# Retention heads ahead of their stick-breaking pair, and a retention head's frames in two halves with the state carried between them

## The chip, the core and the metric

One core of a Trainium2 chip runs one launch of the kernel. The metric is device time in microseconds (us), the median of several runs. TensorE (PE) multiplies matrices, VectorE (DVE) and ScalarE (ACT) do elementwise work, SyncE (SP) issues the weight loads, GpSimd (POOL) issues the other DMAs.

## What is computed

One layer of an encoder for 512 prompt frames and 32 sample frames (544 columns in all), model width 1024, in float32. A normalised input `h` is projected to: queries, keys and values of 4 retention heads (256 wide each), queries, keys and values of 8 stick-breaking heads (128 wide), a gate `rg`, and two branch gates `ga`, `gb`. Merged branches go through an output projection, and an MLP of width 4096 follows. Retention, cut to what the change touches, is

```python
scores = einsum('bihd,bjhd->bhij', q, k) * decay      # inside a chunk of 64 frames, both ways
o      = einsum('bhij,bjhe->bihe', scores, v) + einsum('bihd,bhde->bihe', q, S) * q_decay
S_new  = exp(log_gamma * L) * S + einsum('bjhd,bjhe->bhde', k * k_decay, v)
```

over chunks of 64 frames, with S starting at zero; both `o` and the last S are outputs of the branch. Since the decays multiply, the sum over earlier chunks may be taken directly from keys and values or through a carried S at any frame. A stick-breaking head has exponentials and logarithms in place of a softmax: log-sigmoids of the scores, a reversed cumulative sum over keys (a product with a triangle of -1 on TensorE), an Exp, and the product with the values.

## The kernel before

Everything is kept transposed: features on the 128 partitions, frames in columns. A float32 operand is split into a rounded high part and a rest (`split`: ScalarE copies the high part, VectorE subtracts), and a product is three TensorE products high-high, high-low, low-high (`exact`, `products`). The rounded format is float32r in the code; a plain float32 product runs in two records at a lower rate and is used for blocks of 128 columns.

Weights come as 128 x 1024 tiles, in the order of their use. `load_w` loads one and splits it into `whi` (ScalarE) and `wlo` (VectorE). `gemm` multiplies one such tile with all 544 columns, in two halves of 24 products of 272 columns each; at its start it calls `load_w` for the next tile, whose two buffers are those that the gemm before it has left.

TensorE's order is fixed by the program. The main loop issues gemms, and `Flow` interleaves chains: generators that do the attention work of a head in pieces and yield what they need next (events, PSUM banks, temporaries). `Flow` keeps its own estimate of when engines and buffers are free and lets a piece go, between two k-steps of a gemm, when it holds it to be ready. The order of VectorE and ScalarE is made by a scheduler. Every engine takes its instructions in order, so an instruction that waits holds those behind it.

The stages: first the gemms that read the unnormalised input X while the norm and `h` are made (values of stick-breaking head 0, both value tiles of retention head 0, values of stick-breaking head 1, keys of retention head 0, keys of stick-breaking head 0). Then rounds c = 0 to 3: stick-breaking heads 2c and 2c+1 (gemms, then `sb_chain`), after odd rounds a group of sample frames (`sample_chain`), then retention head c (`retention_chain` for the prompt, `ret_sample_chain` for sample frames, `state_chain` for the final state). Then the gates, 24 gemms with a Sigmoid on ScalarE; after the sixth, `flow.drain()` runs every chain to its end. Output projection and MLP follow.

Names in the steps below. `sc`, `dm`, `dec` are a head's state, its decay table and its key-decay table, loaded by POOL. In `retention_chain` the scores of a 512-frame prompt are computed as blocks of 128 keys by all later queries: 512, 384, 256 and (full precision) 128 columns wide; `pt` holds them masked, `sh`, `sl` their high and low parts, and `values_of` multiplies with the values `rv_hi`, `rv_lo`, `rv_3` in the same widths. In `state_chain`, `kd` are keys times `dec`, transposed to `kt`, and four blocks of 128 frames are multiplied with the values into one bank `sb_`. In `ret_sample_chain` `pd`, `pd_r` are the sample frames' masked scores, `qd` decayed queries, `so` the normalised result that is transposed back. `e` is a stick-breaking head's 128 x 1280 work tile.

```python
    def rstd(sums, n):                       # used by every head
            S.activation(y[:, c], ps, AF.Ln, scale=1.0 / n, bias=epsb)
            S.activation(y[:, c], y[:, c], AF.Exp, scale=-0.5)
        def silu(h, c, p):                   # the gates
            S.activation(sg[:, c], p, AF.Sigmoid)
```

Of the kernel before, what the change touches and what calls it, by code (L numbers as in the profile page):

```python
# [35 lines left out]

MLP_W = 80
OUT_ORDER = (0, 4, 1, 5, 2, 6, 3, 7)

# [6 lines left out]
def constants():  # L46
# [185 lines left out]
def trunk(ctx: ExitStack, tc: tile.TileContext, a: dict, g32):  # L232
# [11 lines left out]
    def tmp():  # L244
        return tp.tile([P, NT], F32, tag="tmp", name="tmp")
# [208 lines left out]
    def query_key_parts(x, n, copy=False):  # L454
# [8 lines left out]
        return hi, lo, last  # L463

    heads = {}

# [63 lines left out]
    with tc.tile_pool(name="xin", bufs=1, side="right") as xp:  # L530
# [54 lines left out]

        flow.wait(vt=2, rv=1, tmp=9, mm=3, at=1)
        vt0, vt1 = sb_value_tiles(), sb_value_tiles()
        rv0, rvs0 = ret_value_tiles()
# [16 lines left out]
        for k in range(KD):  # L605
# [8 lines left out]
        flow.start(value_chain(rc, rv0, P, rvs0, ("rv1", 0)))  # L614
        flow.wait(tmp=1)
        rd = tmp()
        gemm(X, lambda h, c, p: V.scalar_tensor_tensor(
            rd[:, c], p, -1.0 / (2 * D), u[0][:, c], op0=ALU.mult, op1=ALU.mult
        ))
# [6 lines left out]
        rope(X, rk0, turned, 0, 0)  # L626
        flow.give(tmp=2)
        query_key(0, 1, X, u[0])
        flow.until("h", KD - 1)
# [200 lines left out]
    def leave(c):  # L830

        users[c] = users.get(c, 0) + 1
        if users[c] == 3:
            flow.give(rk=1, rq=1, rv=1)

    def retention_chain(c, vt):
# [5 lines left out]
        pt = bigp.tile([P, PACKED], F32, tag="e", name="pt", bufs=2)  # L842
        for bi, blocks in enumerate(GROUPS):
            b_ = bank()
            for n, b in enumerate(blocks):
                _, c0, w = PIECES[b]
                for d in range(2):
                    by_blocks(b_[:, c0 : c0 + w], b, k_r[d], q_r[d], n == 0 and d == 0, d == 1)
            for b in blocks:
                _, c0, w = PIECES[b]  # L850
                o = BANKS[bi][0] + c0
                V.tensor_tensor(pt[:, o : o + w], b_[:, c0 : c0 + w], dm[:, :w], op=ALU.mult)
            flow.give(at=1)
            if bi < 2:
                flow.t = flow.pe
                yield need(at=1)
        flow.give(qk0=1, qk1=1, qk2=1, qk3=1)
# [3 lines left out]
        raw, sq = [], []  # L861
        for ei in range(2):
            ob = bank()
            values_of(ob, vt, slice(ei * P, (ei + 1) * P), parts, pt)
            raw.append(tmp())
            sq.append(tmp())
            S.copy(raw[ei][:, :SEQ], ob)
            S.activation(sq[ei][:, :SEQ], ob, AF.Square)
        flow.give(e=1, sh=1, at=1)
# [12 lines left out]
        leave(c)  # L882
# [43 lines left out]
    def state_chain(c, k, vt, vsamp, sc):  # L926

        dec = bigp.tile([P, NT], F32, tag="dec", name="dec")
        nc.gpsimd.dma_start(out=dec, in_=a["dec"][c])
        yield need(("rqk", c, 0), ("rv0", c), ("rv1", c), ("carried", c), tmp=2)  # L930
        kd = [tmp(), tmp()]
# [5 lines left out]
        for half in (blocks[:4], blocks[4:]):  # L937
# [23 lines left out]
        flow.give(at=1, tmp=2)  # L961
        yield need(at=1)
        sb_ = bank()
# [10 lines left out]
    phase = (cst[:, C_COS:C_SIN], cst[:, C_SIN:C_TRI])  # L974
    for c in range(NH):
        for h in (2 * c, 2 * c + 1):
            for w_col in (1, 0):
                if (h, w_col) != (0, 1):
                    query_key(h, w_col)
            if c == 0:  # L980
                vt = (vt0, vt1)[h]
            else:
                flow.wait(vt=1)
                vt = sb_value_tiles()
                values(H, vt, 0, vs[:, h % 4, :], ("v", h), a["o_v"][h])
            flow.start(sb_chain(h, vt))
        if c % 2:
            flow.start(sample_chain(c // 2))
        x = []
        for n, tag in enumerate(("rk", "rq")):  # L990
            if c == 0 and n == 0:
                x.append(rk0)
                continue
            flow.wait(**{tag: 1})
            x.append(rope_tiles(tag))
            rope(H, x[n], phase, c, n)
        if c == 0:
            rv, rvs = rv0, rvs0
        else:
            flow.wait(rv=1)  # L1000
# [6 lines left out]
        flow.start(ret_sample_chain(c, x[0], x[1], rvs, sc))  # L1007
        flow.start(state_chain(c, x[0], rv, rvs, sc))


# [412 lines left out]
```

## Time and profile before

| | |
|---|---|
| median of 3 runs | 1002.31 us (1002.0 to 1005.52) |
| profiled execution, device time | 1002.26 us |
| its span in the profile | 1000.5 us |
| TensorE busy | 986.7 us, 99% |
| VectorE busy | 668.0 us, 67% |
| ScalarE busy | 522.7 us, 52% |
| granted TensorE clock, mean | 0.998 |
| DMA | 102.71 MB, 103 GB/s |

A row of a timeline gives the start, the duration, engine, line and operation, output tile and inputs, and in brackets the idle time before it with what ended it. Matmuls overlap: what one costs is read from the distance of two starts, not from its duration. `Flow`'s wrapper makes line 225 the line of nearly every instruction, so rows are told apart by tile names.

### The profile page before, as it was taken

The numbers are of one execution on the slowest core, as the hardware profiler recorded it, in microseconds if no ns is written. First come the engines' busy times: TensorE is split into PE (matmuls) and PEld (weight loads), VectorE is DVE, ScalarE is ACT, GpSimd is POOL, SyncE is SP. The second block draws the span as 40 slices with busy tenths as digits, with TensorE's granted clock in tenths as the row PEclk, the third lists the DMA queues.
The fourth block names the chain that finished last, engine by engine and source line by source line (L and its number), as shares of the span: only waits on it lengthen the run. The fifth ranks groups of instructions, "written<-read, shape, count | busy, mean of one in ns | idle before, by whom it ended". The sixth has DMA issues, their size and how long they took to land.

```text
span 1000.5 us, 18622 instructions
## 1 busy us (share of the span) xinstructions
PE 986.7 (99%) x7726; PEld 969.3 (97%) x7726; DVE 668.0 (67%) x1124; ACT 522.7 (52%) x963; POOL 47.2 (5%) x80
## 2 busy tenths in 40 slices
PE   9999999999999999999999999999999999999998
PEld 9999888999999999889999999999999999999998
DVE  7968768866677576756434447974676666676782
ACT  6466756537654675564333335775464445444440
POOL 0000003001000011000000011000000000000000
PEclk9999999999999999999999999999999999999999
DMA  7232224122322135114322245232223332343312
GB/s 253 87 128 75 86 75 149 64 85 96 108 64 85 64 125 164 45 51 165 97 87 85 85 142 185 85 127 85 85 93 101 103 106 87 104 129 96 119 43 90
DMA packets 30932, 102.71 MB, mean 103 GB/s; under 512 B 4096, under 2 KB 6144, under 8 KB 30848
## 3 DMA queue, kind: packets, MB, share of 16 engines
q1 hardware_dynamic: 24768, 80.88, 25.0%
q0 software_dynamic: 6080, 20.65, 6.2%
q8 instruction: 60, 0.98, 0.4%
q14 instruction: 24, 0.20, 0.1%
HBM read 90.51 MB, written 11.01 MB: 101 GB/s over the span
## 4 chain that ended last, share of the span: by engine, by line
PE 95%; ACT 2%; DVE 2%; issue 0%; ACTq 0%; DVEq 0%
PE mm L225 70%; PE at L225 25%; ACT tmp L225 1%; PE at L384 0%; DVE sl L225 0%; ACT e L225 0%; ACT whi L225 0%; ACT L225 0%; DVE tmp L225 0%; ACT kt L225 0%; DVE sh L225 0%; DVE e L225 0%; PE at L600 0%; DVE so L225 0%; ACT st L225 0%
## 5 line engine op out<-in xcount | busy, mean ns | idle before, releaser
L225 PE MATMUL mm<-h_hi,whi 128*128 128x272 f32 x1040 | 304.5, 293 | 0.0
L225 PE MATMUL mm<-h_hi,wlo 128*128 128x272 f32 x1040 | 301.1, 290 | 0.9 <-DVE wlo L225 0.9
L225 PE MATMUL mm<-h_lo,whi 128*128 128x272 f32 x1040 | 300.3, 289 | 0.0
L225 DVE TENSOR_TENSOR wlo<-raw,whi 128x1024 fp32r<-128x1024 f32 (+1 forms) x146 | 167.6, 1150 | 125.8 <-ACT whi L225 125.0
L225 ACT CAST whi<-raw 128x1024 fp32r<-128x1024 f32 (+1 forms) x146 | 144.8, 992 | 179.3 <-PE mm L225 162.1
L225 PEld LDWEIGHTS mm<-h_hi,whi 128*128 128x128 f32 x1040 | 196.7, 189 | 1.9 <-issue 1.3
L225 PEld LDWEIGHTS mm<-h_hi,wlo 128*128 128x128 f32 x1040 | 196.3, 189 | 1.1 <-DVE wlo L225 1.1
L225 PEld LDWEIGHTS mm<-h_lo,whi 128*128 128x128 f32 x1040 | 196.9, 189 | 0.1
L225 PE MATMUL mm<-u_hi,whi 128*128 128x272 f32 x512 | 147.9, 289 | 0.0
L225 PE MATMUL mm<-u_lo,whi 128*128 128x272 f32 x512 | 147.8, 289 | 0.0
L225 PE MATMUL mm<-u_hi,wlo 128*128 128x272 f32 x512 | 147.7, 288 | 0.0
L225 PEld LDWEIGHTS mm<-u_hi,whi 128*128 128x128 f32 x512 | 96.6, 189 | 0.4 <-DVE y L225 0.2
L225 PEld LDWEIGHTS mm<-u_lo,whi 128*128 128x128 f32 x512 | 96.5, 188 | 0.0
L225 PEld LDWEIGHTS mm<-u_hi,wlo 128*128 128x128 f32 x512 | 96.3, 188 | 0.0
L225 PE MATMUL at<-f_hi,wlo 128*128 128x272 f32 x320 | 92.7, 290 | 0.0
L225 PE MATMUL at<-f_lo,whi 128*128 128x272 f32 x320 | 92.2, 288 | 0.0
L225 PE MATMUL at<-f_hi,whi 128*128 128x272 f32 x320 | 92.1, 288 | 0.0
L225 ACT ACTIVATE tmp<-tmp 128x272 f32<-128x272 f32 (+2 forms) x148 | 75.4, 553 | 29.6 <-DVE tmp L225 29.1
L225 DVE TENSOR_TENSOR y<-mm,y 128x272 f32<-128x272 f32 x112 | 48.6, 436 | 29.3 <-PE mm L225 29.3
L225 PEld LDWEIGHTS at<-f_hi,whi 128*128 128x128 f32 x320 | 60.5, 189 | 0.0
L225 PEld LDWEIGHTS at<-f_lo,whi 128*128 128x128 f32 x320 | 60.4, 189 | 0.0
L225 PEld LDWEIGHTS at<-f_hi,wlo 128*128 128x128 f32 x320 | 60.3, 188 | 0.0
(234 smaller groups left out, 1795.0 us busy)
## 6 DMA issues: line engine op xcount, KB each, us to landing
raw<-in_w SPq DMA_DIRECT2D x142, 512.0 KB, 3.5
x<-in_x SPq DMA_DIRECT2D x8, 272.0 KB, 5.2
o_v<-tmp POOLq DMA_DIRECT2D x8, 272.0 KB, 2.4
o_k<-tmp POOLq DMA_DIRECT2D x8, 272.0 KB, 2.5
x<-in_x POOLq DMA_DIRECT2D x8, 272.0 KB, 3.6
o_y<-x POOLq DMA_DIRECT2D x8, 272.0 KB, 2.4
tmp<-o_y POOLq DMA_DIRECT2D x8, 272.0 KB, 3.8
o_y<-y SPq DMA_DIRECT2D x16, 136.0 KB, 1.7
```

What stands on the lines that cost most here:

```text
L225: f(out, *args, **kw)
```

## The change

1. The order of heads is a list, `HEADS`: R0 S0 S1 R1 S2 S3 R2 S4 S5 R3 S6 S7. In the first stage, the values of stick-breaking head 1 and the keys of head 0 make way for the queries of retention head 0. The weights are packed in the new order.
2. A retention head's prompt is treated as two halves of 256 frames. Scores are made inside each half only: 256 columns for its first 128 keys, 128 full-precision ones for the second 128. The later half's queries read the state that the first half leaves: `state_chain` copies the bank after its first two blocks (`mids`), `retention_chain` splits the copy into `sh`, `sl`, multiplies it with the later queries (bank `cx`), and multiplies the result with a decay that stands in the free half of `dm`; it is added to the values' product on VectorE. The final state goes out through `kd[0]` in place of `so_p`.
3. `state_chain` no longer waits for `carried` before its key products but before its update of `sc`; `retention_chain` waits for `mid`.

```diff
+HEADS = "R0 S0 S1 R1 S2 S3 R2 S4 S5 R3 S6 S7".split()
...
+        dm[h, :, 256:] = np.exp(lg[h] * (np.arange(256) - 255))[None]
...
+    def ret_parts(x, n, key):
+
+        hi = qkp.tile([P, SEQ], F32R, tag=f"qk_hi{n}", name=f"qk_hi{n}")
+        lo = qkp.tile([P, SEQ], F32R, tag=f"qk_lo{n}", name=f"qk_lo{n}")
+        src, h, l = x[:, :SEQ], hi, lo
+        if key:
+            src, h, l = (t.rearrange("p (n c) -> p n c", c=256)[:, :, :P] for t in (src, hi, lo))
+        split(src, h, l)
+        return hi, lo, x
...
-        p = 2 - 2 * n
+        p = 2 * n
         yield need(**{f"qk{p}": 1, f"qk{p + 1}": 1})
-        heads["ret", c, n] = [query_key_parts(x[d], p + d) for d in range(2)]
+        heads["ret", c, n] = [ret_parts(x[d], p + d, n == 0) for d in range(2)]
...
-        flow.start(value_chain(rd, vt1, 0, vs[:, 1, :], ("v", 1), a["o_v"][1]))
...
+        rq0 = rope_tiles("rq")
+        rope(X, rq0, turned, 0, 1)
         flow.give(tmp=2)
-        query_key(0, 1, X, u[0])
...
+        pt = bigp.tile([P, PACKED], F32, tag="e", name="pt", bufs=2)[:, : 3 * L]
+        b_ = bank()
+        for i in range(2):
+            for d in range(2):
+                exact(
+                    b_[:, i * L : (i + 1) * L], [t[:, i * L : i * L + P] for t in k_r[d][:2]],
+                    [t[:, i * L : (i + 1) * L] for t in q_r[d][:2]], i == 0 and d == 0, d == 1, **SG,
+                )
+        decayed(b_, 0, L)
...
+                T.matmul(
+                    b_[:, i * P : (i + 1) * P], k_r[d][2][:, s], q_r[d][2][:, s],
+                    start=i == 0 and d == 0, stop=d == 1, **SG,
+                )
+        decayed(b_, 2 * L, P)
...
-        yield need(("rv0", c), ("rv1", c), sh=1, tmp=5, at=2)
-        parts = packed_parts(pt)
+        yield need(("rv0", c), ("rv1", c), ("mid", c), sh=1, tmp=5, at=3)
+        parts = [bigp.tile([P, PACKED + 2 * P], F32R, tag=t, name=t) for t in ("sh", "sl")]
+        M0 = PACKED - SEQ
+        split(mids.pop(c), *[t[:, M0:PACKED] for t in parts])
...
+        cx = bank()
+        for ei in range(2):
+            for d in range(2):
+                o = M0 + d * L + ei * P
+                exact(
+                    cx[:, ei * L : (ei + 1) * L], [t[:, o : o + P] for t in parts],
+                    [t[:, L:] for t in q_r[d][:2]], ei == 0 and d == 0, d == 1, **SG,
+                )
...
+            for b, o, w in ((0, 0, L), (2, L, L), (1, 2 * L, P)):
+                q0 = b * P
+                exact(
+                    ob[:, q0 : q0 + w], [t[:, b, cols] for t in vt[:2]], [t[:, o : o + w] for t in parts],
+                    b == 0, b == 1, **SG,
+                )
+            T.matmul(ob[:, 3 * P :], vt[2][:, cols], pt[:, 2 * L + P :], start=False, stop=True, **SG)
+            S.copy(raw[ei][:, :L], ob[:, :L])
+            V.tensor_tensor(raw[ei][:, L:SEQ], ob[:, L:], carried[:, ei, :], op=ALU.add)
...
-        yield need(("rqk", c, 0), ("rv0", c), ("rv1", c), ("carried", c), tmp=2)
+        yield need(("rqk", c, 0), ("rv0", c), ("rv1", c), tmp=2)
...
-                    [t[:, m, :] for t in vt[:2]], m == 0 and d == 0, m == 3, **SG,
+                    [t[:, m, :] for t in vt[:2]], m == 0 and d == 0, m % 2 == 1, **SG,
                 )
-        so_p = bigp.tile([P, 512], F32, tag="so_p", name="so_p")
+            if c not in mids_made:
+                mids_made.add(c)
+                mids[c] = bigp.tile([P, 512], F32, tag="so_p", name="so_p")
+                S.copy(mids[c], sb_)
+                flow.finish("mid", c)
+        so_p = kd[0][:, :SEQ]
...
-        yield need(at=1)
+        yield need(("carried", c), at=1)
...
+    for kind, n in HEADS:
+        (stick_breaking if kind == "S" else retention)(int(n))
```

What this moves, at three places. First, TensorE, round 0: the end of the first stick-breaking head's cumulative sums (`neg1_r`) and its value products (`vt_hi`, `vt_lo`; the numbers tell buffers apart). Before:

```order
L225 MATMUL at_1111<-sl_1246,tri_r_765 128x256
L225 MATMUL at_1111<-e_1112,neg1_r_767 128x128
L225 MATMUL at_1401<-tmp_r_1332,ones_r_78 128x272
L225 MATMUL at_1401<-tmp_r_1333,ones_r_78 128x272
L225 MATMUL at_1404<-tmp_r_1332,ones_r_78 128x272
L225 MATMUL at_1404<-tmp_r_1333,ones_r_78 128x272
L225 MATMUL at_1425<-tmp_r_1397,ones_r_78 128x272
L225 MATMUL at_1425<-tmp_r_1398,ones_r_78 128x272
L225 MATMUL at_1428<-tmp_r_1397,ones_r_78 128x272
L225 MATMUL at_1428<-tmp_r_1398,ones_r_78 128x272
L225 MATMUL at_1444<-sh_1421,vt_hi_187 128x512
```

Now, after 55 other rows behind the same head's `neg1_r` product:

```order
L229 MATMUL mm_1691<-h_hi_107,whi_1574 128x272
L229 MATMUL mm_1691<-h_lo_108,whi_1574 128x272
L229 MATMUL mm_1691<-h_hi_107,wlo_1575 128x272
L229 MATMUL at_1695<-sh_1625,vt_hi_187 128x512
L229 MATMUL at_1695<-sl_1626,vt_hi_187 128x512
L229 MATMUL at_1695<-sh_1625,vt_lo_188 128x512
```

Eight sums stood between the two steps of the head; now projection matmuls and the next head's scores do.

Second, VectorE after the first stage, in the changed kernel (`tmp_823`, `tmp_824` are `kd`, `wlo` a weight's low part, `at_864` the retention scores):

```order
L229 TENSOR_TENSOR qk_lo3_820<-rq1_597,qk_hi3_819 128x512
L229 TENSOR_TENSOR tmp_823<-rk0_413,dec_771 128x544
L229 TENSOR_TENSOR tmp_824<-rk1_414,dec_771 128x544
L229 TENSOR_TENSOR qd_887<-rq0_596,cst_72 128x32
L229 TENSOR_TENSOR qd_887<-rq1_597,cst_72 128x32
L229 TENSOR_TENSOR wlo_849<-raw_847,whi_848 128x1024
L229 TENSOR_TENSOR tmp_r_907<-tmp_805,tmp_r_906 128x544
L229 TENSOR_TENSOR pt_863<-at_864,dm_769 128x512
L229 TENSOR_TENSOR pd_881<-at_878,cst_72 32x32
L229 TENSOR_TENSOR kt1_897<-at_891,kt0_896 128x512
L229 TENSOR_TENSOR pd_r_882<-pd_881,pd_r_882 32x32
```

Before, the products with `dec` came after the two stick-breaking heads of round 0.

Third, ScalarE in the gates (`at_5502` to `at_5504` are the last head's scores, `mm` a gate's product, `whi_5553` the high part of the weight for the fifth gate gemm). Before:

```order
L225 CAST kt0_5472<-at_5467 128x512
L225 ACT_TABLE_LOAD
L225 ACTIVATE tmp_5479<-at_5476,epsb_80 128x512
L225 ACT_TABLE_LOAD
L225 ACTIVATE tmp_5479<-tmp_5479 128x512
L225 ACTIVATE tmp_5480<-tmp_5479 128x512
L225 COPY so_p_5512<-at_5414 128x512
L225 ACT_TABLE_LOAD
L225 ACTIVATE tmp_5435<-mm_5442 128x272
```

Now:

```order
L229 ACTIVATE e_5505<-at_5503 128x512
L229 ACTIVATE e_5505<-at_5504 128x256
L229 ACT_TABLE_LOAD
L229 ACTIVATE e_5505<-e_5505 128x1280
L229 ACT_TABLE_LOAD
L229 ACTIVATE tmp_5436<-mm_5489 128x272
L229 ACT_TABLE_LOAD
L229 ACTIVATE e_5505<-e_5505 128x1280
L229 CAST whi_5553<-raw_5552 128x1024
L229 ACT_TABLE_LOAD
```

From the first gate to the end of the chains there were 4 table loads and there are 13.

## Rows read from the trace of the kernel before

**Rows 1.** The page, part 1: busy us, share of the span and instructions of each engine.

```profile
PE 986.7 (99%) x7726; PEld 969.3 (97%) x7726; DVE 668.0 (67%) x1124; ACT 522.7 (52%) x963; POOL 47.2 (5%) x80
```

**Rows 2.** TensorE's waits: waiting line, releaser, us in total, times, longest us.

```profile
PE at L225 <- ACT kt L225: 2.0, 1, 2.0
PE at L225 <- DVE so L225: 1.9, 3, 1.3
```

**Rows 3.** Windows: stretch, its length, busy us and instructions of each engine, granted clock, DMA share, GB/s.

```profile
75.00:160.00 85.00, 79.12 (x585) 74.62 (x584) 61.49 (x118) 54.42 (x124) 6.13 (x11) 1.00 0.23 76
160.00:400.00 240.00, 239.32 (x1869) 231.48 (x1869) 169.05 (x309) 142.07 (x294) 22.87 (x34) 1.00 0.32 103
400.00:440.00 40.00, 39.62 (x334) 35.95 (x333) 27.16 (x52) 21.53 (x48) 0.00 (x0) 1.00 0.13 41
440.00:460.00 20.00, 17.97 (x132) 17.64 (x130) 10.78 (x15) 12.29 (x19) 1.44 (x2) 0.91 0.39 132
...
452.00:454.00 2.00, 2.00 (x12) 2.00 (x12) 2.00 (x4) 0.00 (x0) 0.32 (x1) 0.56 0.54 129
```

**Rows 4.** TensorE's timeline, value products of retention head 0 and the first key-value products behind them: start us, duration us, what.

```profile
149.92 0.39 PE L225 MATMUL at<-sh,rv_lo 128*128 128x512 f32 x1
150.15 0.34 PE L225 MATMUL at<-sh,rv_hi 128*128 128x384 f32 x1
150.32 0.34 PE L225 MATMUL at<-sl,rv_hi 128*128 128x384 f32 x1
150.50 0.34 PE L225 MATMUL at<-sh,rv_lo 128*128 128x384 f32 x1
...
150.91 0.28 PE L225 MATMUL at<-sh,rv_lo 128*128 128x256 f32 x1
151.03 0.38 PE L225 MATMUL at<-pt,rv 128*128 128x128 f32 x2
151.17 0.36 PE L225 MATMUL at<-rv_hi,kt 128*128 128x256 f32 x1
151.37 0.28 PE L225 MATMUL at<-rv_lo,kt 128*128 128x256 f32 x1
```

**Rows 5.** TensorE's timeline, its opening (20 rounded products of 128 columns) and the change from the first stage (x) to the gemms on h.

```profile
1.32 4.53 PE L384 MATMUL at<-ones_r 128*128 128x128 f32 x20 [1.32 <-DVE ones_r L333]
...
6.79 0.43 PE L225 MATMUL mm<-x_lo,whi 128*128 128x272 f32 x1
7.02 0.43 PE L225 MATMUL mm<-x_hi,wlo 128*128 128x272 f32 x1
...
54.69 0.28 PE L225 MATMUL mm<-h_hi,whi 128*128 128x272 f32 x1
54.81 0.29 PE L225 MATMUL mm<-h_lo,whi 128*128 128x272 f32 x1
```

**Rows 6.** TensorE's timeline in round 0, the first value products of stick-breaking head 0.

```profile
106.83 0.47 PE L225 MATMUL at<-sh,vt_hi 128*128 128x512 f32 x1 [0.32 <-DVE sh L225]
108.33 0.51 PE L225 MATMUL at<-sl,vt_hi 128*128 128x512 f32 x1 [1.03 <-DVE sl L225]
```

**Rows 7.** GpSimd's timeline, the first loads of a retention head's tables, and from the DMA view of 50 to 65 us the row of one of them (KB each, median us from issue to landing).

```profile
55.45 0.72 POOL L1005 DMA_DIRECT2D sc<-in_state  x1 [17.34 <-DVE neg_r L646]
...
56.73 0.54 POOL L929 DMA_DIRECT2D dec<-in_dec  x1
...
dec<-in_dec POOLq DMA_DIRECT2D x1, 272.0 KB, 5.6
```

**Rows 8.** ScalarE's timeline in the drain: a logarithm and an exponential of retention head 3 among the gates.

```profile
442.94 1.28 ACT L225 ACT_TABLE_LOAD   x1
444.23 0.69 ACT L225 ACTIVATE tmp<-at,epsb 128x512 f32<-128x512 f32 x1
444.93 1.28 ACT L225 ACT_TABLE_LOAD   x1
```

**Rows 9.** ScalarE's and VectorE's timelines, a stick-breaking head's scores: absolute values, Exp, Ln, and VectorE's three sums.

```profile
82.02 0.87 ACT L225 ACTIVATE e<-at 128x512 f32<-128x512 f32 x2 [0.16 <-PE at L225]
...
83.15 1.28 ACT L225 ACTIVATE e<-e 128x1280 f32<-128x1280 f32 x1
...
84.64 1.27 ACT L225 ACTIVATE e<-e 128x1280 f32<-128x1280 f32 x1
...
85.94 1.62 DVE L225 SCALAR_TENSOR_TENSOR e<-at,e 128x512 f32<-128x512 f32 x3 [1.90 <-ACT e L225]
```

**Rows 10.** TensorE's timeline in round 1: the sample frames' product and the transposes of its normalised result.

```profile
219.28 0.30 PE L225 MATMUL at<-rvs,pd_r 96*32 96x256 f32 x1
...
221.80 0.31 PE L225 MATMUL at<-cst,so 32*128 32x32 f32 x2
```

**Rows 11.** TensorE's timeline in the drain: a gate's product and the last key-value product of the sample state.

```profile
449.01 0.29 PE L225 MATMUL mm<-h_hi,wlo 128*128 128x272 f32 x1
451.33 0.50 PE L225 MATMUL at<-rvs,kt 96*128 96x256 f32 x2 [2.03 <-ACT kt L225]
```

**Rows 12.** VectorE's timeline at the end of the first stage: two operations of 544 columns, one of 1024, and the next.

```profile
49.55 1.35 DVE L225 TENSOR_TENSOR rk<-rk,tmp 128x544 f32<-128x544 f32 x2
50.82 1.22 DVE L225 TENSOR_TENSOR wlo<-raw,whi 128x1024 fp32r<-128x1024 f32 x1
51.96 0.72 DVE L225 TENSOR_TENSOR h_lo<-tmp,h_hi 128x544 fp32r<-128x544 f32 x1
```

More of the change, by code (lines that the diff above doesn't have):

```diff
@@ L584, in first_norm @@
             flow.give(tmp=6)
-        flow.wait(vt=2, rv=1, tmp=9, mm=3, at=1)
-        vt0, vt1 = sb_value_tiles(), sb_value_tiles()
+        flow.wait(vt=1, rv=1, tmp=9, mm=3, at=1)
+        vt0 = sb_value_tiles()
         rv0, rvs0 = ret_value_tiles()
@@ L626, in trunk @@
         rope(X, rk0, turned, 0, 0)
+        flow.wait(rq=1)
+        rq0 = rope_tiles("rq")
+        rope(X, rq0, turned, 0, 1)
         flow.give(tmp=2)
-        query_key(0, 1, X, u[0])
         flow.until("h", KD - 1)
@@ L834, in leave @@
             flow.give(rk=1, rq=1, rv=1)
+    mids, mids_made = {}, set()
     def retention_chain(c, vt):
@@ L840, in retention_chain @@
         k_r, q_r = heads.pop(("ret", c, 0)), heads.pop(("ret", c, 1))
[L842 to L855, printed above, removed]
-                yield need(at=1)
@@ new lines, in retention_chain @@
+        b_ = bank()
[6 more added lines that the diff above has]
+        decayed(b_, 0, L)
+        flow.give(at=1)
+        flow.t = flow.pe
+        yield need(at=1)
+        b_ = bank()[:, :L]
+        for i in range(2):
+            s = slice(i * L + P, (i + 1) * L)
+            for d in range(2):
[3 more added lines that the diff above has]
+                )
@@ new lines, in retention_chain @@
+        decayed(b_, 2 * L, P)
+        flow.give(at=1, qk0=1, qk1=1)
+        yield need(("rv0", c), ("rv1", c), ("mid", c), sh=1, tmp=5, at=3)
+        parts = [bigp.tile([P, PACKED + 2 * P], F32R, tag=t, name=t) for t in ("sh", "sl")]
+        M0 = PACKED - SEQ
+        split(mids.pop(c), *[t[:, M0:PACKED] for t in parts])
+        V.tensor_copy(parts[0][:, : 2 * L + P], pt[:, : 2 * L + P])
+        V.tensor_tensor(
+            parts[1][:, : 2 * L + P], pt[:, : 2 * L + P], parts[0][:, : 2 * L + P].bitcast(F32), op=ALU.subtract
+        )
@@ new lines, in retention_chain @@
+        yield need()
+        cx = bank()
+        for ei in range(2):
+            for d in range(2):
+                o = M0 + d * L + ei * P
[3 more added lines that the diff above has]
+                )
+        flow.give(qk2=1, qk3=1)
+        raw, sq = [tmp(), tmp()], [tmp(), tmp()]
+        carried = pair(sq[1][:, :SEQ], L)
+        later = dm[:, L:].rearrange("p (o c) -> p o c", o=1).to_broadcast([P, 2, L])
@@ L862, in retention_chain @@
+        V.tensor_tensor(carried, pair(cx, L), later, op=ALU.mult)
+        obs = []
         for ei in range(2):
             ob = bank()
[L864 to L869, printed above, removed]
+            cols = slice(ei * P, (ei + 1) * P)
+            for b, o, w in ((0, 0, L), (2, L, L), (1, 2 * L, P)):
[3 more added lines that the diff above has]
+                    b == 0, b == 1, **SG,
+                )
+            T.matmul(ob[:, 3 * P :], vt[2][:, cols], pt[:, 2 * L + P :], start=False, stop=True, **SG)
+            S.copy(raw[ei][:, :L], ob[:, :L])
+            V.tensor_tensor(raw[ei][:, L:SEQ], ob[:, L:], carried[:, ei, :], op=ALU.add)
@@ L870, in retention_chain @@
+        for ei in range(2):
+            S.activation(sq[ei][:, :SEQ], raw[ei][:, :SEQ], AF.Square)
+        flow.give(e=1, sh=1, at=2)
         V.tensor_tensor(sq[0][:, :SEQ], sq[0][:, :SEQ], sq[1][:, :SEQ], op=ALU.add)
@@ L974, in trunk, with stick_breaking, retention @@
     phase = (cst[:, C_COS:C_SIN], cst[:, C_SIN:C_TRI])
[L975 to L996, printed above, removed]
+    def stick_breaking(h):
+        for w_col in (1, 0):
+            query_key(h, w_col)
+        if h == 0:
+            vt = vt0
+        else:
+            flow.wait(vt=1)
+            vt = sb_value_tiles()
+            values(H, vt, 0, vs[:, h % 4, :], ("v", h), a["o_v"][h])
+        flow.start(sb_chain(h, vt))
+        if h % 4 == 3:
+            flow.start(sample_chain(h // 4))
+    def retention(c):
         if c == 0:
-            rv, rvs = rv0, rvs0
+            k, q, rv, rvs = rk0, rq0, rv0, rvs0
         else:
+            flow.wait(rk=1)
+            k = rope_tiles("rk")
+            rope(H, k, phase, c, 0)
+            flow.wait(rq=1)
+            q = rope_tiles("rq")
+            rope(H, q, phase, c, 1)
             flow.wait(rv=1)
@@ L1006, in trunk @@
         flow.start(retention_chain(c, rv))
-        flow.start(ret_sample_chain(c, x[0], x[1], rvs, sc))
-        flow.start(state_chain(c, x[0], rv, rvs, sc))
+        flow.start(ret_sample_chain(c, k, q, rvs, sc))
+        flow.start(state_chain(c, k, rv, rvs, sc))
+    for kind, n in HEADS:
+        (stick_breaking if kind == "S" else retention)(int(n))
     mp = ctx.enter_context(ExitStack())
@@ L1351 @@
     ws = []
-    ws += [sv[0], rv[0], rv[1], sv[1], rk[0], rk[1]]
-    for c in range(NH):
-        for h in (2 * c, 2 * c + 1):
-            ws += [sk[h], sq[h], sv[h]][: 2 if c == 0 else 3]
-        for p in (rk, rq, rv) if c else (rq,):
-            ws += [p[2 * c], p[2 * c + 1]]
+    ws += [sv[0], rv[0], rv[1], rk[0], rk[1], rq[0], rq[1]]
+    for kind, n in HEADS:
+        n = int(n)
+        if kind == "S":
+            ws += [sk[n], sq[n], sv[n]] if n else [sk[n], sq[n]]
+        elif n:
+            ws += [p[2 * n + i] for p in (rk, rq, rv) for i in range(2)]
     for t in range(KD):
```

14 lines of the change are left out of this document (6 added, 8 removed).

## The prediction

> **What bounds it now.** I read the page's busy line first: TensorE works 986.7 of 1000.5 us [rows 1], so only two things can move the time: the work on TensorE itself, and the 14 us in which it waits. Then TensorE's waits [rows 2], to see whom it waits for, and the windows [rows 3], to see where: 5.88 us idle (85.00 less 79.12) between 75 and 160 us, 0.68 between 160 and 400, 0.38 between 400 and 440. The reader should see that nearly all of it lies in the first two rounds of heads and in the last microseconds before the chains are drained. Behind both I read timelines. At 104 to 109 us dependent pieces stand back to back: the value products of the first stick-breaking head wait for its high and low parts [rows 6]. At 449.01 TensorE stops until 451.33 [rows 11], and from 452 to 454 the granted clock is 0.56 of full speed, so 1.2 GHz for most of it [rows 3].
>
> The sum is made against the profiled execution, 1002.26 us (span 1000.5); the median of the runs, 1002.31, is the same to 0.1.
>
> **1. TensorE's own work: -3.3 us.** From starts that follow each other, a moving operand of 512 columns costs 0.23 us, 384 costs 0.175 (two in 0.35), 256 costs 0.12, and the full-precision one of 128 (two records) 0.22: 0.34 from 151.03 to 151.37, less the 0.12 of the one behind it [rows 4]. A retention head had, in scores and values together, 12 each of 512, 384 and 256 and 4 full-precision ones: 12 x 0.525 + 0.88 = 7.18 us. Now it has 36 of 256 (12 scores, 12 on the carried state, 12 values), 6 full-precision ones and 6 rounded ones of 128 columns: 4.32 + 1.32 + 6 w. The trace before has w only in its opening: 20 in 4.53 us, 0.22 each, while a 272-column one takes 0.23 there against 0.12 to 0.13 later (54.69 to 54.81), so at the level of 1.2 GHz [rows 5]. At 2.4 GHz that is 0.11; I take 0.12, the price of 256 columns. That makes 6.36 us, 0.82 less a head, 3.3 less for four. The ends: w = 0.06, half of the 256-column row, gives -4.7; w = 0.22, the full-precision row, gives -0.9. The Trainium skill (TensorE: Matmul & The Clock Gate, Back-to-back issue gap) gives about 81 ns for 128 columns in a stream of weight loads and matmuls. By that the term would be -4.2; the opening row speaks for more than 81 ns.
>
> **2. The waits of the first two rounds: -7.3 us.** 5.88 us idle [rows 3], and about 0.16 more for each of some nine waits, because idle time is counted from a modelled end: the last matmul of a run is shown 0.29 long although the next one could start after 0.126 [rows 5]. In the new order these places have projection matmuls between dependent pieces (58 rows between the cumulative sums of the first stick-breaking head and its values, where eight short ones stood). One cover is thin: the wait for a weight's low part at 90 us. The new gap between that head's scores and the gemm in question is 10 us where it was 7, so I let it go too. Nothing gone is one end of this term, all gone the other.
>
> **3. Round 0 waits for its tables: +1.6 us.** State, decay and key-decay tables are loaded into memory that the first stage's tiles leave, so they are issued 0.8 us after its last product (55.45 against 54.69), one after another, the key decay last at 56.73, landing 5.6 us later [rows 5, 7]. Before, nobody needed them until 115 us. Now the retention head runs at once. The first stage ends 0.5 us earlier (a value tile's transposes stand elsewhere), so the key decay lands at about 61.8. VectorE stands at the key-decay products from about 59.3. Behind them in order: the two products 1.28, a weight's low part 1.14, a low part 0.64 [rows 12], the masked scores 0.6, transposed keys 0.6 and four small ones 0.5 with one copy on ScalarE between (sizes scaled from the same rows). The small masked scores of the sample frames are ready at 66.8; TensorE comes for them at 54.2 + 57 projection matmuls + the scores and transposes in between = 65.2. So 1.6. If the load takes 3 us as the two ahead of it did, 0; if all three queue behind weight loads, 4.
>
> **4. The sample frames' normalisation: +0.9, less 1.1.** From their product to the transposes of the result takes 2.5 us (219.28 to 221.80) with ScalarE and VectorE free [rows 10]. Rounds 1 and 2 now give it 12 matmuls and four transposes, 2.1 us: 0.43 each. Rounds 0 and 3 give it 2.4 or more. What TensorE waited between 160 and 440 us before (0.68 and 0.38) goes. Bounds: 0 and 3.
>
> **5. The drain: -4.0 and +6.8 us.** Before, the last chain was a retention head; its wait at 449.01 cost 2.2 us [rows 11], and the clock afterwards 1.8 (0.91 granted over 20 us) [rows 3]. Both go. Now the last two stick-breaking heads and the second sample group run while the gates are made, and their exponentials and logarithms alternate with the gates' sigmoids on ScalarE. Each change of function costs a table load of 1.29 us, and a logarithm followed by an exponential costs two [rows 8]. The order of the changed kernel has 13 loads there, the one before 4: 11.6 us more. The costliest place: from the last head's scores ScalarE does the last absolute values 0.9, load, Exp 1.28, load, a sigmoid 0.3, load, Ln 1.27 [rows 8, 9], and only then VectorE the three of 1.62 [rows 9] and the low part of the next weight, 1.14 [rows 12]: 10.4 us. TensorE has 62 projection matmuls until it needs that weight: 7.85. So 2.5 us stall. Directly behind it the sample scores (1.3 us) must pass absolute values, a load and an Exp on ScalarE before the casts for this head's cumulative sums: 6 us against TensorE's 3.1, and I count 2.5 more. The later loads lie beside 60 matmuls each. The earlier stall, 2.2 us, brought the clock down; two of 2.5 within 6 us I count as bringing it down once, 1.8. Bounds: 0 (VectorE and ScalarE ahead of plan) and 12 (the same shortfall at the other two places, the clock twice).
>
> Pool queue, weights and everything behind the drain are the same work; I cost them at nothing, TensorE being gapless there before.
>
> Sum: -3.3 - 7.3 + 1.6 + 0.9 - 1.1 - 4.0 + 6.8 = -6.4: **995.9 us**, 0.6% less.
>
> **Rivals.**
> *The drain hides its loads.* If TensorE reaches the last scores late enough, the +6.8 falls away: 989.1. For it: even between 440 and 460 us ScalarE was busy for only 61% (12.29 of 20) [rows 3]. Against it: the loads stand in one dependent chain, so idle time of ScalarE elsewhere does not help.
> *The early waits come back.* VectorE is at 72% between 75 and 160 us [rows 3] and the change takes little from it; if half of the 7.3 reappears between new neighbours: 999.5.
> *The 128-column products cost full-precision time*, against the opening row: 998.3.
> *Slower: ScalarE bounds the drain.* Its work from the first gate to the end of the chains is 13 loads, 16.8 us, and some 29 us of casts, sigmoids and chain work, against 48 us of TensorE work there. If each switch also stretches the hop around it, TensorE follows ScalarE and the drain costs 12 instead of 6.8, with a clock drop at both stalls; and the early waits come back whole: 995.9 + 5.2 + 7.3 = 1008.4; with half of them 1004.8. It decides from 13 us of new stalls on. The Trainium skill (ScalarE: Activation LUTs, Table sets) has the rule behind it: batch calls by set. Its section on the cost of a load gives 2.66 us a switch; by that the chain of three loads would be 4.1 us longer. It also says that one set serves Ln and Exp; the trace shows a load between them [rows 8], so here the switches are more than the page's rule makes them, and each is cheaper than its price.
>
> **Chances.** Forecast 0.50 (993 to 999.5); drain hidden 0.15; early waits back 0.18; 128-column price 0.07; slower rival 0.10. The range leaves out most of the last and the far half of the second: 990 to 1002. What can be told from no change is 0.5%, 5 us: under 997.3 lie two thirds of the forecast's chance, all of the hidden drain and little of the rest, 0.52; over 1007.3 half of the slower rival, 0.05; 0.43 between.
>
> **What would show it.** In the changed profile: TensorE's busy time 3 us less; retention score, carried and value products of 256 columns 0.12 apart and those of 128 columns too (term 1); no idle time between 85 and 160 us (2); one wait of 1 to 2 us at about 65 us, VectorE standing until the key decay lands (3); waits of 0.3 us for the sample result in rounds 1 and 2 (4); two waits of 2 to 3 us between 430 and 445 us, the first for a weight's low part, the second for the parts of the stick-breaking sums, and a granted clock under 1 once behind them (5). I am wrong if TensorE's idle time between 75 and 160 us stays over 3 us, or if the drain shows no wait, or more than 8 us of them.

## The result and the profile after

The changed kernel takes 994.96 us (median of 993.16, 995.25, 994.67 and 995.89) beside 1002.45 for the kernel before on the same chip: ratio 0.9917, 95% interval [0.9892, 0.9941]. On a second chip it was 995.22 against 1004.54: 0.9906 [0.9891, 0.9921]. Single executions far slower, such as one of 1050.88 us at a granted clock of 0.852 on the second chip, are left out of the ratios. The prediction said 995.9 in a range of 990 to 1002.

The busy line, TensorE's waits (waiting line, releaser, us in total, times, longest) and the windows (length, busy us and instructions of PE, PEld, DVE, ACT, POOL, granted clock, DMA share, GB/s) of the first profile after, span 991.4 us:

```profile
PE 980.4 (99%) x7766; PEld 966.3 (97%) x7766; DVE 667.9 (67%) x1128; ACT 536.6 (54%) x984; POOL 45.6 (5%) x80
```

```profile
PE at L229 <- ACT sh L229: 2.2, 1, 2.2
...
PE at L229 <- DVE so L229: 0.9, 3, 0.4
```

```profile
55.00:75.00 20.00, 20.00 (x161) 18.84 (x160) 16.55 (x37) 12.55 (x30) 3.62 (x6) 1.00 0.35 112
75.00:160.00 85.00, 84.64 (x657) 82.25 (x655) 63.39 (x118) 50.80 (x109) 3.65 (x7) 1.00 0.27 87
160.00:400.00 240.00, 239.46 (x1923) 233.36 (x1923) 166.11 (x305) 147.75 (x324) 18.32 (x29) 1.00 0.29 93
440.00:460.00 20.00, 15.62 (x130) 13.96 (x130) 15.25 (x25) 17.37 (x26) 0.00 (x0) 1.00 0.16 54
```

Against [rows 3]: the 5.88 us idle between 75 and 160 us are 0.36. Between 440 and 460 us there are 4.38 idle where there were 2.03, at a granted clock of 1.00 where it was 0.91. TensorE is busy 6.3 us less than in [rows 1]; part of that is work, part is that waits lengthen the modelled end of the matmul ahead of them, and part is the stretch at the lower clock that the kernel before had in its profile.

TensorE's timeline, value products of a retention head in its new form (start, duration, what):

```profile
170.18 0.28 PE L229 MATMUL at<-sh,rv_lo 128*128 128x256 f32 x1
170.30 0.22 PE L229 MATMUL at<-sh,rv_hi 128*128 128x128 f32 x1
170.36 0.27 PE L229 MATMUL at<-sl,rv_hi 128*128 128x128 f32 x1
170.47 0.28 PE L229 MATMUL at<-sh,rv_lo 128*128 128x128 f32 x1
170.58 0.44 PE L229 MATMUL at<-pt,rv 128*128 128x128 f32 x2
```

Read the distance between starts, not the durations: the 256-column product at 170.18 costs 0.12, as in [rows 4]; of the three with 128 columns the first costs 0.06 and the other two 0.11, 0.093 on average.

The first round: when GpSimd issued the load of the key decay, and VectorE's wait for it:

```profile
56.67 0.54 POOL L983 DMA_DIRECT2D dec<-in_dec  x1
```

```profile
60.59 1.36 DVE L229 TENSOR_TENSOR tmp<-rk,dec 128x544 f32<-128x544 f32 x2 [0.73 <-DMA dec<-in_dec]
```

The issue time is that of [rows 7] to 0.1 us, but the decay is used 3.9 us after its issue, not 5.6. VectorE lost 0.73 us to it and TensorE nothing: in the window from 55 to 75 us it is busy for 20.00 of 20.

The drain (the stretch at the gates in which all chains run to their end): ScalarE's timeline, and the three places at which TensorE stopped. The first two are one stall, for the high and then the low part of the same weight. The number in brackets is the idle time ahead, with its releaser:

```profile
435.03 1.28 ACT L229 ACT_TABLE_LOAD   x1
...
437.62 1.28 ACT L229 ACT_TABLE_LOAD   x1
438.91 0.40 ACT L229 ACTIVATE tmp<-mm 128x272 f32<-128x272 f32 x1
439.33 1.28 ACT L229 ACT_TABLE_LOAD   x1
440.62 1.27 ACT L229 ACTIVATE e<-e 128x1280 f32<-128x1280 f32 x1
441.80 1.03 ACT L229 CAST whi<-raw 128x1024 fp32r<-128x1024 f32 x1
```

```profile
441.71 0.28 PE L229 MATMUL mm<-h_hi,wlo 128*128 128x272 f32 x1
442.88 0.39 PE L229 MATMUL mm<-h_hi,whi 128*128 128x272 f32 x1 [0.88 <-ACT whi L229]
...
444.74 0.39 PE L229 MATMUL mm<-h_hi,wlo 128*128 128x272 f32 x1 [1.33 <-DVE wlo L229]
...
447.62 0.44 PE L229 MATMUL at<-sl,tri_r 128*128 128x512 f32 x1
450.22 0.44 PE L229 MATMUL at<-sh,neg_r 128*128 128x384 f32 x1 [2.16 <-ACT sh L229]
```

In ScalarE's rows the exponential, a gate's sigmoid and the logarithm take turns, and each brings its table: three loads in the 6.8 us between the last scores and the cast of the next weight. TensorE needs that weight at 441.84 (441.71 and 0.13 for the matmul there) and gets its high part at 442.88 and its low part at 444.74: 1.04 and 1.50 us, once the matmul in between is taken off. The second stall, 447.62 to 450.22, is 2.37 us beyond its 512 columns.

### The profile page after: what moved, and what is told of

Same layout as the page of the kernel before. It is cut to its first block, busy times and chain, and to the rows that moved or that the text cites. A ratio compares the mean times of both kernels' runs of the same rounds, so it can differ in the third digit from the quotient of the medians.

```text
span 991.4 us, 18729 instructions
## 1 busy us (share of the span) xinstructions
PE 980.4 (99%) x7766; PEld 966.3 (97%) x7766; DVE 667.9 (67%) x1128; ACT 536.6 (54%) x984; POOL 45.6 (5%) x80
## 4 chain that ended last, share of the span: by engine, by line
PE 96%; ACT 2%; DVE 1%; DMA 1%; issue 0%; ACTq 0%; DVEq 0%
PE mm L229 70%; PE at L229 25%; DMA x<-in_x 1%; ACT L229 1%; PE at L388 0%; ACT e L229 0%; DVE wlo L229 0%; ACT tmp L229 0%; ACT st L229 0%; PE at L614 0%; DVE so L229 0%; ACT so L229 0%; ACT whi L229 0%; DVE st L229 0%; DVE e L229 0%
## 5 line engine op out<-in xcount | busy, mean ns | idle before, releaser
L229 ACT ACTIVATE tmp<-tmp 128x544 f32<-128x544 f32 (+2 forms) x154 | 78.5, 555 | 27.3 <-DVE tmp L229 26.8
```

The source lines that it names most:

```text
L229: f(out, *args, **kw)
```

## The experiments

The theory after the result: the new order takes the early waits away, the halves shorten TensorE's work, and the drain gives some of it back through table loads. The rivals: it is all the halves' doing, or the drain's stalls have nothing to do with the loads.

**Order alone, halves alone.** The first kernel has the new order of heads and of the first stage with the old retention function; the second has the new retention function in the old order:

```
order alone:   HEADS and the first stage as changed; retention_chain, its key and
               query parts, and the state product as before
halves alone:  order and first stage as before; ret_parts, retention_chain and the
               middle state as changed (keys in qk2, qk3, queries in qk0, qk1)
```

> The new order of heads and of the first stage, with the old retention (one triangle of 512 frames). Theory, that the early waits go because of the order: TensorE idle under 1 us between 85 and 160 us, TensorE's busy time 3.5 to 4 us more than the changed kernel's, two stalls in the drain as there; 997.5 to 1000 us. Rival 1, that finer retention pieces fill the early waits and the order does not: idle time of 4 to 6 us between 75 and 160 us, 1000 to 1004 us. Rival 2, that the halves cost as much as they save: 994 to 996 us, like the changed kernel.

> Two halves with a carried state in the old order (two stick-breaking heads, then the retention head) and the old first stage. Theory: only TensorE's work shrinks, by 3.3 to 3.9 us, the idle time of 5.9 us between 75 and 160 us stays, and the drain is the old one with its stall of 2.2 us; 998 to 1000 us. If the new wait of the carried state for the state of the first half shows, up to 2 us more. Rival, that the whole gain of 7.5 us is in the halves: 995 to 996 us with the early idle time gone. Rival, that the 128-column products cost as much as they save: 1001 to 1003 us.

Measured: order alone 1013.99 us, ratio 1.0098 [1.0084, 1.0112]; halves alone 1002.35, 0.9984 [0.9975, 0.9993]; both, in the same runs:

> The changed kernel as it is, as the reference for the other runs of this series. 994.5 to 996 us, ratio to the kernel before 0.992 to 0.994. If the profile shows a stretch at the lower granted clock in the drain (about 440 to 460 us), the run is 1.7 to 2 us over the 993.2 of the first profile, which had none.

995.22, 0.9906 [0.9891, 0.9921]: the time as expected, the ratio just under it. So the parts don't add: +9.5 us for the one and -2.2 for the other, and -9.3 for both. Neither time was what the theory expected: order alone is outside every range, and halves alone landed where its second rival had put it (128-column products that cost what they save); the windows show why that reading does not hold. Order alone, then halves alone:

```profile
85.00:160.00 75.00, 75.00 (x572) 72.57 (x570) 59.68 (x110) 45.40 (x99) 3.82 (x6) 1.00 0.29 93
160.00:400.00 240.00, 231.92 (x1786) 222.43 (x1785) 156.94 (x283) 136.45 (x293) 16.57 (x26) 0.99 0.26 85
...
460.00:480.00 20.00, 13.26 (x99) 11.88 (x100) 8.51 (x16) 13.85 (x22) 0.00 (x0) 0.74 0.16 54
```

```profile
85.00:160.00 75.00, 70.53 (x525) 67.27 (x523) 52.50 (x99) 46.65 (x108) 5.74 (x9) 0.98 0.26 86
...
400.00:440.00 40.00, 34.68 (x293) 31.69 (x292) 23.14 (x45) 20.86 (x44) 0.00 (x0) 0.92 0.12 40
```

The early idle time between 85 and 160 us follows the order: none with the new one, 4.47 us with the old one, whatever the retention. What was not foreseen stands further on: order alone is idle for 8.08 us between 160 and 400 us, and for 6.74 between 460 and 480 at a clock of 0.74. Halves alone is idle for 5.32 between 400 and 440. That last one is a single wait, and ScalarE's timeline shows it to be the drain's trouble again, for a piece of the retention head this time: the sample frames' normalisation (so, st) waits for three loads:

```profile
427.76 0.37 ACT L227 ACTIVATE so<-at 32x256 f32<-32x256 f32 x1 [3.04 <-PE at L227]
...
428.24 1.28 ACT L227 ACT_TABLE_LOAD   x1
...
429.95 1.28 ACT L227 ACT_TABLE_LOAD   x1
431.25 0.29 ACT L227 ACTIVATE st<-st,epsb 32x1 f32<-32x1 f32 x1
...
432.02 1.28 ACT L227 ACT_TABLE_LOAD   x1
```

**No loads in the drain.** To take the drain out of the comparison, the sigmoids of the first two gate steps were made from functions of the table that the chains use:

```diff
+    def sigmoid(out, x, t):
+        if t >= 2:
+            S.activation(out, x, AF.Sigmoid)
+            return
+        S.activation(out, x, AF.Exp, scale=-1.0)
+        S.activation(out, out, AF.Ln, bias=1.0)
+        S.activation(out, out, AF.Exp, scale=-1.0)
```

> The changed kernel with the sigmoids of the first two gate steps made from Exp, Ln and Exp, so that ScalarE has no table load between the first gate and the end of the chains (there were 12). Theory, that the drain's two stalls (2.5 and 2.7 us) hang on the chain of loads: both gone or under 1 us together, no clock under 1 there, 5 us less than the changed kernel: 988.5 to 991 us. Rival, that the stalls come from the weight parts and the sample scores being late whatever ScalarE loads (24 more activations of 0.3 to 0.4 us stand there instead): 993 to 996 us, with the two stalls still at the first and second weight after the last scores.

Measured: 989.63 us, 0.9853 [0.9839, 0.9866], 5.6 us less than the changed kernel in the same runs; all its runs had a mean granted clock of 1.0, where those of the changed kernel that are compared had 0.997 and 0.998. Between 390 and 480 us ScalarE's timeline has 1 load instead of 13. TensorE's waits between 440 and 460 us:

```profile
443.19 0.39 PE L229 MATMUL mm<-h_hi,wlo 128*128 128x272 f32 x1 [0.31 <-DVE wlo L229]
449.41 0.45 PE L229 MATMUL at<-sh,neg_r 128*128 128x384 f32 x1 [0.99 <-ACT sh L229]
```

The first stall is all but gone, the second is halved, and the clock behind them holds. The stalls hang on the loads, though not the whole of the second: 1 us of it stays, over the expected total by a little.

The same edit in the other three kernels:

> The new order with the old 512-frame retention, and no table loads in the first two gate steps. The order alone measured 1014.0 with stalls of about 10 us and the lower clock behind 440 us. Theory, that this part hangs on the loads and the rest (waits of 8 us between 160 and 400 us, 4 us more TensorE work than the halves have) does not: 998 to 1002 us. Rival, that the old retention is late everywhere and the drain only shows it: 1006 to 1014 us.

> The kernel before with the sigmoids of the first two gate steps made from Exp, Ln and Exp (no table load between the first gate and the end of the chains; it had 4). Theory: only its last stall (2.2 us) and the clock drop behind it (about 2) go: 3 to 4.5 us under the kernel before, ratio 0.9955 to 0.997. Rival, that the 24 extra activations cost as much: ratio 0.999 to 1.002.

> Two halves in the old order, without table loads in the first two gate steps. With the loads it measured 1002.35, with a wait of 5.3 us for the sample frames' normalisation behind three loads at 429 us and a granted clock of 0.84 there. Theory, that this wait ate the saving of the halves: it goes, 994 to 997 us, that is 3 to 5 us under the kernel before with the same edit. Rival, that the halves save nothing in the old order: within 1.5 us of the kernel before with the same edit, 999 to 1001 us.

| no loads in the first two gate steps | old retention | two halves |
|---|---|---|
| old order | 1000.37, 0.9961 [0.9948, 0.9974] | 997.29, 0.9929 [0.9915, 0.9944] |
| new order | 1004.56, 1.0002 [0.9992, 1.0011] | 989.63, 0.9853 [0.9839, 0.9866] |

The four ran on three chips, on which the kernel before took 1004.5 to 1004.9 us. In the kernel before, the edit gives 4.5 us, as expected: from 440 to 460 us TensorE is now busy for 20.00 of 20 at a clock of 1.00. With the drain out of the way the halves in the old order give 3.1 us (997.29, just over the expected 994 to 997). That is the size of their saving of work, but not shown to be it alone: the profile with the halves has more idle time, 8.84 us against 6.96 from 55 to 480 us, and a higher mean clock, 1.000 against 0.996. With the loads the wait of 5.1 us hid part of the gain. The new order gives 7.7 us with the halves and costs 4.2 without them; of the 7.7, 4.4 are idle time between 75 and 160 us (4.73 to 0.36) and 2.3 idle time behind it. The old retention in the new order came out at 1004.56, between the two expectations: the waits between 160 and 400 us (8.06) are those that the theory left in, but one of the drain's stayed, 2.65 us for the second group of sample frames, with a clock of 0.91 from 460 to 480 us. The profiled spans of the two kernels in the lower row are 1003.5 and 987.8. Of these 15.7 us, 3.3 are the work of four heads as priced; 8.7 are idle time (10.9 against 2.2 us, summed over the windows from 55 to 480 us); and about 4 the clock (0.996 of 1003.5 against 1.000; most of its other executions had 0.998). TensorE's waits of the first of them, the upper line being both groups of sample frames:

```profile
PE at L227 <- ACT tmp L227: 6.1, 2, 3.4
PE at L227 <- DVE so L227: 3.3, 4, 1.4
```

They are the same pieces that wait briefly or not at all in the changed kernel. One of them was followed in the order-alone run, the sample result of round 1, where TensorE waited 1.40 us instead of 0.36. ScalarE's timeline there:

```profile
158.28 0.37 ACT L227 ACTIVATE so<-at 32x256 f32<-32x256 f32 x1 [2.53 <-PE at L227]
...
158.66 0.39 ACT L227 COPY tmp<-mm 128x272 f32<-128x272 f32 x1
158.94 0.29 ACT L227 ACTIVATE st<-st,epsb 32x1 f32<-32x1 f32 x1
...
159.42 0.18 ACT L227 ACTIVATE st<-st 32x1 f32<-32x1 f32 x1
159.51 0.56 ACT L227 CAST kt<-at 128x512 fp32r<-128x512 f32 x1
```

A gemm's copies and the cast of the transposed keys stand between the steps of the normalisation, and VectorE then does the keys' low part (160.10) ahead of its own steps (from 160.71). In the changed kernel the copies lie ahead of the first step (155.65 and 155.93 us, the step at 156.86) and the keys' low part behind the last (158.92). From the first step to the result it takes 3.25 us in the one and 2.13 in the other. TensorE's cover is the same in both, 12 projection matmuls and four transposes, 2.1 us, so what differs is the company that each piece happens to get. Whether the other waits have the same cause was not tried.

**Which stall belongs to what.** Three edits on the changed kernel. First, the weight parts ahead of everything else in the first two gate steps:

```diff
-        load_w()
+        with tc.high_priority() if first[0] else ExitStack():
+            load_w()
```

> The changed kernel with the cast and the low part of each weight tile put ahead of ScalarE's and VectorE's other work in the first two gate steps (the same table loads but one fewer). Theory, that the drain's two stalls are one late chain: the first stall (2.5 us, for the weight's high and low part) goes, TensorE then reaches the second place 2.5 us earlier while ScalarE gets there about 0.5 us earlier, so the second stall (2.7 us) grows to 4 to 5: 994 to 996 us, no more than 1 us under the changed kernel. Rival, that the stalls are independent: the second stays at 2.7 and 2.5 us are saved, with the clock held perhaps 4: 991 to 993 us.

> The kernel with the weight parts first in the first two gate steps, which measured 996.0, once more for its profile. Theory, one late chain: no wait for a weight part between 435 and 446 us, and one wait of 4 to 5 us for the parts of the stick-breaking sums behind the sample scores, at about 445 to 450 us; ScalarE busy without a gap over 0.5 us from the last scores' absolute values to the cast that ends it. Rival: that wait stays at 2.7 us and the time was lost elsewhere.

Measured: 995.99, 0.9915 [0.9898, 0.9931], no gain; the second run took 994.82, and its TensorE waits in the drain are

```profile
442.47 0.40 PE L229 MATMUL mm<-h_hi,whi 128*128 128x272 f32 x1 [0.89 <-ACT tmp L229]
446.08 0.50 PE L229 MATMUL at<-sh,tri_r 128*128 128x512 f32 x1 [0.74 <-DVE sh L229]
447.83 0.49 PE L229 MATMUL at<-sl,tri_r 128*128 128x512 f32 x1 [1.25 <-DVE sl L229]
450.18 0.69 PE L229 MATMUL at<-sh,neg_r 128*128 128x384 f32 x1 [1.86 <-ACT sh L229]
```

No weight is waited for any more, and TensorE still gets past the second place at 450.18 (450.22 before the edit; up to 448 us both profiles have a clock of 1.00). The 2.5 us reappear as waits for the last head's parts (3.85 us idle where there were 2.16) and as one for a free accumulator, whose sigmoid now stands behind the logarithm. It is one late chain, as expected, though not the single wait of 4 to 5 us; ScalarE's idle time in it was 1.09 us at one place, the wait for TensorE's sample scores, so it is not gapless.

Second, the last retention head behind the last two stick-breaking heads:

```diff
-HEADS = "R0 S0 S1 R1 S2 S3 R2 S4 S5 R3 S6 S7".split()
+HEADS = "R0 S0 S1 R1 S2 S3 R2 S4 S5 S6 S7 R3".split()
```

> The changed kernel with the last retention head behind the last two stick-breaking heads instead of ahead of them; nothing else. ScalarE has 4 table loads between the first gate and the end of the chains, not 12. Theory, that the order of the last three heads made the drain's stalls: the two stalls of 5.2 us go, and what halves in the old order showed at the end, a wait of about 5 us for the sample frames' normalisation behind the gates' sigmoids, comes instead; 993 to 997 us, no gain. Rival, that the drain only has to be rid of loads: stalls under 2.5 us in all, 990 to 992 us.

> Both edits: the last retention head at the end, and no table loads in the first two gate steps. Theory: without loads the last head's kind matters little, 988 to 991 us, within 1.5 us of the kernel with one table alone (989.6). Rival, that the retention head at the end has waits of its own, by its carried state: 991 to 994 us.

Measured: 997.77, 0.9938 [0.9923, 0.9952], just over the expected range, and without loads 993.26, 0.9889 [0.9872, 0.9907], in the range of its rival. The drain's stalls were exchanged for the wait of the sample result, with 7 loads between 390 and 480 us (the 4 of the expectation were too few):

```profile
430.51 0.28 PE L229 MATMUL at<-cst,so 32*128 32x32 f32 x2 [3.39 <-DVE so L229]
```

The edit without loads is 3.6 us over the same without this move. Its TensorE waits name the cost: three new ones of 1.1 us between 325 and 395 us, in the middle of the program, where two stick-breaking pairs now follow each other:

```profile
PE at L229 <- ACT tmp L229: 1.1, 1, 1.1
PE at L229 <- DVE tmp_r L229: 1.1, 1, 1.1
...
PE at L229 <- ACT s_all L229: 1.1, 1, 1.1
```

Third, no loads and two pieces put later by the planner:

```diff
         V.tensor_scalar(so, ob[:DEC, :256], st[:, 3:4], None, op0=ALU.mult)
         flow.give(at=1)
+        flow.t += 700
         yield need(at=1)
...
         later_parts(e, parts)
+        if h == 7:
+            flow.t += 1500
         yield need()
```

> The changed kernel without table loads in the first two gate steps, and with two pieces put later in TensorE's order by the planner: 0.7 us more behind every sample product before its result is transposed (cover 2.7 to 3.0 us instead of 2.0 to 2.4), 1.5 us more before the last head's cumulative sums. Theory, that the remaining stalls are cover that is short by a little: the three waits for the sample result (1.4 us) and the one for the sums (1.2 to 1.7) go, 986 to 988 us against 989.6. Rival, that the pieces moved later make others late: 988.5 to 991 us.

Measured: 987.12, 0.9827 [0.9809, 0.9845], the fastest of all. The waits for the sample result and for the sums are gone, and at the head of its list stand the opening's wait, which every kernel has, and a weight part:

```profile
PE at L388 <- DVE ones_r L337: 1.3, 1, 1.3
PE mm L229 <- DVE wlo L229: 0.3, 1, 0.3
...
```

The 2.5 us are what these waits had cost: cover that was 0.3 to 0.5 us short three times and 1.2 short once.

## Why the prediction was right

The time came out 0.9 us from the forecast, and the forecast's case is the one that happened; but one term (the tables of round 0) did not come, and one (the early waits) was right only under a condition that the prediction did not state.

**1. TensorE's work, -3.3.** Right. The 128-column product costs 0.093 instead of 0.12, which makes the term -3.9. The no-loads pair in the old order measures 3.1, with the reservation made there. The 81 ns that the Trainium skill states for 128 columns (TensorE: Matmul & The Clock Gate, Back-to-back issue gap) is none of the three distances here, 0.06 for the one that shares its weights with the next and 0.11 for the other two.

**2. The early waits, -7.3.** Right in place and size: 0.36 us idle is left of 5.88, and that is a wait for a sample result, of term 4. The 1.4 us added for the modelled ends were not measured by themselves. What the prediction did not state is that this term needs the halves. With the old retention the same order costs 4.2 us, since other waits come between 160 and 480 us. The rival "the early waits come back" thus named a real danger, but looked for it in VectorE's load between 75 and 160 us; the one wait that was followed is lengthened on ScalarE and on VectorE, by about half each.

**3. The tables of round 0, +1.6.** Failed, at both ends of the comparison. The load took 3.9 us where the one row of the kernel before that has this transfer gives 5.6 [rows 7], so the decay was used at 60.59 and not at 61.8, and the sample frames' masked scores were ready at 65.78 instead of 66.8. And TensorE came for them at 66.77, not at 65.2. VectorE's row and TensorE's:

```profile
65.60 0.18 DVE L229 TENSOR_TENSOR pd_r<-pd,pd_r 32x32 fp32r<-32x32 f32 x1
```

```profile
66.77 0.30 PE L229 MATMUL at<-rvs,pd_r 96*32 96x256 f32 x1
```

The first stage ended at 54.63 and not at 54.2, and 63 projection matmuls lie ahead of that product, six more than were counted. With a decay 1.2 us later the wait would have been about 0.2 us by these rows (an estimate), so the load time alone does not explain the 1.6. The lower end, 0, had been given for a load as short as the two ahead of it.

**4. The sample frames' result, +0.9 and -1.1.** Nearly. Three waits of 0.53, 0.53 and 0.34 us, 1.4 beyond the matmul ahead of them, where two of 0.43 were priced; round 3 was given too much cover. What was waited between 160 and 440 us before went, as said: the 0.54 left there are these waits.

**5. The drain, -4.0 and +6.8.** Right by its mechanism, its places in the program and its sizes: 2.5 and 2.4 us where 2.5 and 2.5 were worked out, the first for the weight parts, the second for the parts of the sums. Against the places in time that were given, 430 to 445 us, the second came late, at 447.62 to 450.22. The part of 1.8 for the clock was not in the first profile, which held 1.00 throughout. In the second it was there, behind the first stall and ahead of the end of the second (0.78 from 444 to 446 us; then, in windows of two us of that run):

```profile
446.00:448.00 2.00, 2.00 (x10) 1.99 (x9) 2.00 (x3) 0.70 (x1) 0.00 (x0) 0.50 0.63 215
448.00:450.00 2.00, 2.00 (x27) 0.85 (x25) 1.97 (x4) 0.40 (x1) 0.00 (x0) 0.50 0.12 47
450.00:452.00 2.00, 1.49 (x6) 0.50 (x2) 0.25 (x1) 1.58 (x2) 0.00 (x0) 0.51 0.61 195
```

Half the clock is the 1.2 GHz level. From the first product on h to the first of the output projection that run takes 522.76 us (55.58 to 578.34) and the first one 520.71 (54.63 to 575.34): 2.05 more for the clock, near the 1.8. Six of the seven executions compared show a mean clock under 1, so this belongs to the kernel, and the first profile is the exception. The kernel without loads held 1.0 in all of its runs, which shows that the drop hangs on these stalls. Over the same stretch it takes 517.47 us, so of its 5.6 us about 3.2 are the stalls and 2 the clock. The advice to group activations by table set, and the set that holds Exp and Ln together (the Trainium skill, ScalarE: Activation LUTs, Rules for kernel authors), is borne out: without the sigmoids, Exp and Ln alternate from 390 to 480 us with one load.

Not in the prediction: one wait of 0.6 us for the residual input (x) at 585 us in the output projection. It is not in the second profile.

The forecast was close partly because errors cancelled. By the terms, against the first profile: 0.6 more from the work, 1.6 from the tables and 1.8 from the clock made it faster, 0.5 of sample waits and 0.6 of the residual slower, -2.9 in all; the profiled execution was 993.16, 2.7 under the forecast. With the clock drop, as in most runs, about 2 of it come back. That the time came within 0.9 us is in part luck.

## What to carry to other kernels

Where a planner lays pieces between matmuls, price an order and the size of its pieces together: here each of the two edits alone gave 2.2 us or lost 9.5, and both gave 9.3. When work with Exp and Ln is moved beside work with another table's function, count the table loads in each dependent chain; ScalarE's busy share of the kernel before (61% from 440 to 460 us) did not show them, and in the changed kernel it is 87% there (17.37 of 20); building the other function from the resident table can cost less than the loads. And if making one late piece early saves nothing, follow the chain to the next thing that its engine owes before giving up on the stall.

## What the runs showed that was not expected

The granted clock behind the first of the drain's stalls fell to 0.50 for about 6 us in one execution and stayed at 1.00 in another of the same kernel, so a single profile does not tell whether a stall of 2.5 us costs the clock as well. The waits of the first rounds can cost it too: in the run of the kernel before without loads, whose first rounds are the same program, 85 to 160 us was at 0.98, while [rows 3] of the kernel before have 1.00 there. And of three 128-column products with the same moving width, the one whose successor uses the same weights cost half of the others.
